# A two-layer diffusion backbone on one core: generated state-space weights made earlier, in joined operations, with fewer transfers

## The chip, the cores and the metric

One core of one Trainium2 chip runs the whole program. The metric is the device time of one execution in microseconds (us). Before the change the median of three runs is 1579.98 us (1578.12 to 1581.42). Times of the trace are counted from the first instruction.

## The reference

The model has width 1024, 512 latent tokens and 256 context tokens, and two post-norm layers. Layer 0 is windowed attention (16 query heads, 4 key heads, 128 wide), layer 1 a bidirectional state-space mixer (S5): 128 groups of 16 channels, each with 64 complex states and two directions, followed by a gated linear unit. In both layers the input projection also yields a gate path z, and the output is projected back and normalised:

```python
for i in range(DEPTH):
    h = x * (1.0 + scale) + shift            # the same for the context hc
    pz = h @ w_in
    p, z = pz[..., :-E_WIDTH], pz[..., -E_WIDTH:]
    y = attention_mixer(p) if i == 0 else s5_mixer(p)
    x = layer_norm(alpha * x + gate * ((y * silu(z)) @ w_out[i]))
# inside s5_mixer, for each direction rev:
abar = exp(lam * dt); bbar = ((abar - 1.0) / lam)[..., None] * bmat
h_t = abar * h_{t-1} + bbar @ u_t            # complex, per group
y = d * u + sum over rev of real(cmat @ h_t)
```

The parameters of the state-space layer (lam, step, B, C, D) are inputs, so the matrices made of them must be computed in the kernel.

## The kernel before, in words

**Numbers.** Large products are made of three passes in a reduced format: each operand is split into a high and a low part (`load_split`, lines 138 to 147: ScalarE rounds, VectorE subtracts), and `mm3` (lines 153 to 157) does high x high, high x low, low x high. A projection weight is loaded as one 512 KB chunk (`wchunk`, line 149) by SyncE at line 144, with two buffers for the raw chunk and two each for the parts.

**The state-space layer by chunks of 8 tokens.** Inside a chunk the recurrence is unrolled, so the kernel needs three families of matrices made from the parameters, the generated weights. All are written to DRAM and read back in layer 1:
- `gen_w` (lines 856 to 877), 64 weights: the input of a chunk to its state. One weight loads, for each direction, the tiles gE (from esc, line 865) and gB (from bt, line 867), makes two products (lines 873, 874) and a difference and a sum (lines 875, 876), and stores gW to wsc (line 877). POOL (the GpSimd engine) computes all of it. gE and gB have three buffers each, gW two.
- `gen_o` (lines 880 to 937), 32 weights of two groups each: state to output. It loads gcb and gpp, makes by, bx and bb (lines 900 to 902), and for each direction o and x and their sum (lines 912 to 914), which goes to osc in two stores a direction (line 918). POOL does it, but for q < 14 every fourth q goes to VectorE (`DO`, `DQ`).
- `lag`, inside `gen_o` (lines 920 to 936): the products of state-to-output with input-to-state for the 15 lags inside a chunk, on TensorE (lines 927 to 929, three matmuls for each of four column groups of 32; each matmul is two instructions in the trace). ScalarE and VectorE copy the result to gK, VectorE adds the D term in line 933, and it goes to ksc (line 934). Every eighth q starts 8 transfers that spread it to m0sc.

The tables esc and ppsc, which these read, come from `discretise` and `powers` (lines 713 to 853), whose arithmetic runs on VectorE in the first 190 us, beside the modulation (`ada_first`, `ada_late`) and the first projections.

**Where it runs.** `main` (lines 1315 to 1532) traces the attention layer (`layer0`) as 48 steps n, one per head pair and block of 128 tokens, plus what is needed ahead of it: `head(0)`, the first key, value and query projections in ten pieces, beside which `ada_late` loads modulation weights and multiplies with them. After each step `bg(n)` adds background work. Step 0 finishes `discretise`; steps 1 to 27 hold the 64 gen_w; steps 28 to 47 hold 14 gen_o. The next 10 gen_o are added in the first five calls of `side` during layer 0's output projection (`outproj0`), the last 8 in the first three blocks of `instate`, where layer 1 makes its chunk states from wsc. Each lag product is traced one gen_o late. Layer 1's `outstate` reads osc and m0sc.

**What sets the order.** A planner orders the instructions of each engine when the program is built: it plays the program with a model of durations and takes, on each engine, the ready instruction of best priority. `tc.high_priority(offset=-80)` (GP) puts the background 80 instructions back, -50 (LP) the lag products. The engines then execute their queues strictly in that order, and SyncE's queue, which issues nearly all transfers (the weights of line 144 and those of gen_w and gen_o alike), waits at each transfer for what that transfer needs.

Of the kernel before, what the change touches and what calls it, by code (L numbers as in the profile page):

```python
# [44 lines left out]
def prep(x, c, ctx, c_ctx, ada_w, ada_b, ln_g, ln_b, w_out, attn_w_in, attn_sink,  # L45
         s5_w_in, s5_lam_re, s5_lam_im, s5_log_step, s5_b_re, s5_b_im, s5_c_re, s5_c_im,
         s5_d, s5_glu_w, s5_glu_b, **_):
    a = consts()
# [53 lines left out]
    a["bt"] = bt.transpose(3, 1, 5, 0, 2, 4)  # L102
# [5 lines left out]
    a["cb"] = np.concatenate([a["cb"].reshape(32, 128, 512), dd], 2)  # L108
# [25 lines left out]
class K:  # L134
# [197 lines left out]
def layer0(k, bg, late):  # L332
# [380 lines left out]
def discretise(k, pool, sub):  # L713
# [56 lines left out]
    with sub("disc2") as p:  # L770
# [6 lines left out]
        for d in range(2):  # L777
            for t0 in (0, 4):
# [13 lines left out]
                for r in range(2):  # L792
                    for h in range(2):
                        nc.sync.dma_start(k.esc[d, t0:t0 + 4, :, r, h].rearrange("t i p -> i t p"),
                                          Et[64 * h:64 * h + 64, :, r, :])
# [60 lines left out]
def gen_w(k, pool, i):  # L856

    nc, a = k.nc, k.a
    eng = nc.vector if i % DW == DW - 1 else nc.gpsimd
    W = pool.tile([128, 2, 2, 2, 64], F32, name="gW", bufs=2)  # L860
    for d in range(2):
        E = pool.tile([128, 2, 2, 64], F32, name="gE", bufs=3)
        B = pool.tile([128, 2, 2, 64], F32, name="gB", bufs=3)
        e = k.esc[d, 0, i]
        nc.sync.dma_start(E, bass.AP(tensor=e.tensor, offset=e.offset, ap=[[64 * 256, 8], [0, 16], [1, 256]]))
        b = a["bt"][i, d]
        nc.sync.dma_start(B, bass.AP(tensor=b.tensor, offset=b.offset, ap=[[0, 8], [256, 16], [1, 256]]))
        m1 = pool.tile([128, 2, 2, 64], F32, name="gm1", bufs=2)
        m2 = pool.tile([128, 2, 2, 64], F32, name="gm2", bufs=2)

        def eb(r):
            return E[:, r][:, None].to_broadcast([128, 2, 2, 64])
        eng.tensor_tensor(m1, B, eb(0), op=ALU.mult)  # L873
        eng.tensor_tensor(m2, B, eb(1), op=ALU.mult)  # L874
        eng.tensor_tensor(W[:, d, :, 0], m1[:, 0], m2[:, 1], op=ALU.subtract)  # L875
        eng.tensor_tensor(W[:, d, :, 1], m1[:, 1], m2[:, 0], op=ALU.add)
    nc.sync.dma_start(k.wsc[i], W.rearrange("p d a r q -> p d (a r q)"))


def gen_o(k, pool, q):  # L880
# [4 lines left out]
    cbd = pool.tile([128, 528], F32, name="gcb", bufs=2)  # L885
    nc.sync.dma_start(cbd, a["cb"][q])
    cb = cbd[:, 0:512].rearrange("p (t d g n) -> p t d g n", t=4, d=2, g=4)
    pp = pool.tile([128, 2, 80], F32, name="gpp", bufs=2)
    nc.sync.dma_start(pp, k.ppsc[q])
    O = []  # L890
    bb = pool.tile([128, 8, 2, 16], F32, name="gbb", bufs=2)
    by = pool.tile([128, 2, 4, 16], F32, name="gby")
    bx = pool.tile([128, 2, 4, 16], F32, name="gbx")
# [9 lines left out]
    for d in range(2):  # L903
        o = pool.tile([128, 4, 9, 16], F32, name="gO", bufs=3)
        x = pool.tile([128, 4, 9, 16], F32, name="gX", bufs=1)

        def cc(t):
            return cb[:, t, d][:, :, None].to_broadcast([128, 4, 9, 16])

        def pb(o_):  # L910
            return pp[:, d, o_:o_ + 36].rearrange("p (g k) -> p g k", g=4)[:, :, :, None].to_broadcast([128, 4, 9, 16])
        eng.tensor_tensor(o, cc(0), pb(0), op=ALU.mult)  # L912
        eng.tensor_tensor(x, cc(1), pb(36), op=ALU.mult)  # L913
        eng.tensor_tensor(o, o, x, op=ALU.add)  # L914
# [5 lines left out]
    def lag():  # L920
# [16 lines left out]
    return lag  # L937
# [11 lines left out]
def gen_dram(k, dp, kind=None):  # L949
    k.esc = dp.tile([2, 8, 64, 2, 2, 64], F32, name="esc")  # L950
    k.ppsc = dp.tile([32, 128, 2, 80], F32, name="ppsc")
    k.wsc = dp.tile([64, 128, 2, 256], F32, name="wsc")
    k.osc = dp.tile([64, 128, 2, 2, 128], F32, name="osc")
# [185 lines left out]
def outstate(k, ib, X, ahead=None):  # L1139
# [4 lines left out]
    for g4 in range(0, 8, 4):  # L1144
        ps = k.ps.tile([128, 4, 128], F32, name="yps", tag="yp", bufs=2)
        for j in range(4):
# [5 lines left out]
            nc.sync.dma_start(O, k.osc[ib * 8 + g4 + j])  # L1152
# [152 lines left out]
N0, NW = 1, 28  # L1305
QO, QN = 24, 3
QA, NB = 14, 5
# [7 lines left out]
def main(tc, a):  # L1315
# [14 lines left out]
    with contextlib.ExitStack() as es:  # L1330
# [16 lines left out]
        with contextlib.ExitStack() as e2:  # L1347
# [34 lines left out]
            k.qp = Q("qp")  # L1382
            lags = []


            def out_q(upto, flush):
                nonlocal nq
                while nq < upto:
# [3 lines left out]
                    if len(lags) > 1:  # L1392
                        with tc.high_priority(offset=-LP):
                            lags.pop(0)()
                while flush and lags:
                    lags.pop(0)()

            def bg(n):
# [6 lines left out]
                elif n < NW:  # L1405
# [3 lines left out]
                    for i in range((n - N0) * 64 // (NW - N0), (n - N0 + 1) * 64 // (NW - N0)):  # L1409
                        with tc.high_priority(offset=-GP):  # L1410
                            gen_w(k, gw, i)
# [5 lines left out]
            layer0(k, bg, k.ada_late())  # L1417
# [8 lines left out]
        with contextlib.ExitStack() as e2:  # L1426
# [10 lines left out]
            gw = opener(e4)("go2", side="right")  # L1437
            nb = 0
# [111 lines left out]
```

## Time and profile before

| | before |
|---|---|
| median of 3 runs | 1579.98 us |
| the profiled execution, own time | 1584.47 us |
| its span, first to last instruction | 1582.7 us |
| TensorE (PE) busy | 1440.4 us (91%) |
| VectorE (DVE) busy | 1031.6 us (65%) |
| ScalarE (ACT) busy | 647.4 us (41%) |
| POOL busy | 650.3 us (41%) |
| mean granted clock of TensorE | 0.958 |
| DMA, hardware queue of SyncE | 59.0% of 16 engines' span |

Busy time is the union of the instructions of an engine; matmuls overlap, so a busy TensorE is not one at its peak. The clock is a share of full speed (2.4 GHz); in the records it is 1.0 or 0.5 in each stretch, 0.5 being 1.2 GHz. A wait is idle time of an engine ahead of an instruction, with the instruction that ended it. The first 90 us are the modulation and the first projections, to 706 us runs the attention layer, to 912 its output projection, to about 1164 the states of layer 1, and then the rest of layer 1.

### The profile page before, as it was taken

To read this page: it belongs to the slowest core of one execution; us is meant where nothing else is said; L and a number is where in the kernel's file an instruction comes from. 1 tells how busy PE (TensorE), PEld (TensorE's weight loads), DVE (VectorE), ACT (ScalarE), POOL (GpSimd) and SP (SyncE) were. 2 spreads that over 40 slices of the span, in tenths; PEclk is the share of its full clock that TensorE was granted. 3 is DMA by queue.
4 is the path that set the end of the run, shared out by engine and by line. 5 is a ranking of instruction groups with operands and counts; after the bars stand their busy time and mean duration, and the time that the engine had idled before them with its cause. 6 is when DMAs were issued, how large, how long until landed. Compare 5 with 4: busy or idle time off the path is not lost.

```text
span 1582.7 us, 26680 instructions
## 1 busy us (share of the span) xinstructions
PE 1440.4 (91%) x9348; PEld 1169.9 (74%) x9348; DVE 1031.6 (65%) x2679; ACT 647.4 (41%) x1256; POOL 650.3 (41%) x798
## 2 busy tenths in 40 slices
PE   7999999988997949978989799979989989999997
PEld 2545889977886848866767787768878767788876
DVE  7744666763655437775659920988888987565466
ACT  1211656644455425452223324334557355343220
POOL 0000079888999876655885545520000000000230
PEclk9999999998998969999999899989999999999999
DMA  9665455555565553587686477687766876655541
GB/s 338 213 197 177 96 168 181 183 175 183 169 191 189 168 163 120 159 242 212 185 254 193 147 244 224 198 245 240 241 212 198 288 253 221 212 187 168 184 150 57
DMA packets 270789, 309.64 MB, mean 196 GB/s; under 512 B 47296, under 2 KB 186176, under 8 KB 270656
## 3 DMA queue, kind: packets, MB, share of 16 engines
q1 hardware_dynamic: 245312, 295.37, 59.0%
q10 hardware_dynamic: 25344, 12.59, 2.8%
q8 instruction: 73, 1.20, 0.3%
q14 instruction: 60, 0.49, 0.1%
HBM read 239.20 MB, written 77.07 MB: 200 GB/s over the span
## 4 chain that ended last, share of the span: by engine, by line
PE 50%; DMA 18%; DVE 11%; POOL 10%; issue 4%; ACT 4%; SPq 2%; DVEq 0%; POOLq 0%; ACTq 0%
DMA wsc<-gW 3%; PE pg L155 3%; PE adaps L166 3%; PE pg L157 3%; PE pg L156 3%; DMA wr<-wout 3%; PE ins L1056 3%; DMA gB<-bt 2%; POOL gm L873 2%; POOL gm L874 2%; DMA gr<-gsc 2%; PE yps L1114 2%; ACT X L1099 2%; PE pq L156 2%; PE pq L155 2%
## 5 line engine op out<-in xcount | busy, mean ns | idle before, releaser
L146 DVE TENSOR_TENSOR wl<-wr,wh 128x1024 fp32r<-128x1024 f32 x104 | 132.0, 1270 | 183.0 <-ACT wh L145 182.7
L145 ACT ACTIVATE wh<-wr 128x1024 fp32r<-128x1024 f32 x104 | 109.9, 1058 | 263.5 <-DMA wr<-w 75.7
L1290 POOL TENSOR_TENSOR xt<-xt,lng 128x512 f32<-128x512 f32 (+1 forms) x9 | 12.8, 1431 | 488.1 <-DMA xt<-n0sc 488.1
L873 POOL TENSOR_TENSOR gm<-gB,gE 128x256 f32<-128x256 f32 x128 | 110.2, 861 | 185.1 <-DMA gB<-bt 185.0
L155 PE MATMUL pg<-ga,wh 128*128 128x512 f32 x256 | 100.7, 393 | 1.9 <-ACT wh L145 1.9
L874 POOL TENSOR_TENSOR gm<-gB,gE 128x256 f32<-128x256 f32 x128 | 101.7, 795 | 0.0
L157 PE MATMUL pg<-ga,wl 128*128 128x512 f32 x256 | 100.6, 393 | 0.5 <-DVE wl L146 0.5
L914 POOL TENSOR_TENSOR gO<-gO,gX 128x576 f32<-128x576 f32 x58 | 92.6, 1596 | 2.2
L912 POOL TENSOR_TENSOR gO<-gcb,gpp 128x576 f32<-128x576 f32 x58 | 75.5, 1304 | 27.1 <-PE lag L927 19.3
L1079 DVE TENSOR_TENSOR x<-m 128x64 f32<-128x64 f32 x376 | 82.5, 239 | 2.5
L488 DVE TENSOR_TENSOR ptl<-PT,pth 128x512 fp32r<-128x512 f32 (+1 forms) x96 | 60.7, 639 | 33.3 <-ACT pth L487 32.7
L913 POOL TENSOR_TENSOR gX<-gcb,gpp 128x576 f32<-128x576 f32 x58 | 78.5, 1354 | 1.9
L875 POOL TENSOR_TENSOR gW<-gm,gm 128x128 f32<-128x128 f32 x128 | 71.0, 555 | 14.9 <-DMA wsc<-gW 14.4
L927 PE MATMUL lag<-gO,gbb 128*32 128x128 f32 x256 | 42.8, 313 | 36.0 <-POOL gO L914 31.2
L462 ACT ACTIVATE P<-P,nm 128x512 f32<-128x512 f32 (+1 forms) x64 | 49.5, 774 | 62.6 <-DVE nm L446 62.3
L900 POOL TENSOR_TENSOR gby<-gcb,gpp 128x128 f32<-128x128 f32 x29 | 14.4, 496 | 147.1 <-DMA gcb<-cb 94.3
L484 PE MATMUL PT<-ident,P 128*128 128x128 f32 x352 | 61.8, 287 | 8.3 <-DVE vl L389 5.1
L146 DVE TENSOR_TENSOR gl<-gr,gh 128x512 fp32r<-128x512 f32 x48 | 49.4, 1033 | 28.6 <-ACT gh L145 28.6
L155 PE MATMUL pq<-hh,wh 128*128 128x512 f32 x160 | 65.5, 410 | 2.8 <-ACT hh L256 2.8
L468 ACT ACTIVATE P<-P,es 128x512 f32<-128x512 f32 (+2 forms) x96 | 60.9, 681 | 15.4 <-DVE es L466 15.0
L155 PE MATMUL S<-kh,qh 128*128 128x256 f32 (+1 forms) x160 | 51.9, 325 | 15.6 <-DVE nm L446 9.3
L156 PE MATMUL pq<-hl,wh 128*128 128x512 f32 x160 | 65.3, 408 | 0.8 <-DVE hl L257 0.8
(314 smaller groups left out, 4853.6 us busy)
## 6 DMA issues: line engine op xcount, KB each, us to landing
wr<-w SPq DMA_DIRECT2D x40, 512.0 KB
gE<-esc SPq DMA_DIRECT2D x128, 128.0 KB
gB<-bt SPq DMA_DIRECT2D x128, 128.0 KB
wsc<-gW SPq DMA_DIRECT2D x64, 256.0 KB
osc<-gO SPq DMA_DIRECT2D x128, 128.0 KB
wr<-wout SPq DMA_DIRECT2D x32, 512.0 KB
W<-wsc SPq DMA_DIRECT2D x32, 512.0 KB
om<-osc SPq DMA_DIRECT2D x64, 256.0 KB
```

The source lines that it names most:

```text
L145: nc.scalar.activation(hi, raw, AF.Copy)
L146: nc.vector.tensor_sub(lo, raw, f32(hi))
L155: mm(out, wh, mh, start=start, stop=False)
L156: mm(out, wh, ml, start=False, stop=False)
L157: mm(out, wl, mh, start=False, stop=stop)
L873: eng.tensor_tensor(m1, B, eb(0), op=ALU.mult)
L874: eng.tensor_tensor(m2, B, eb(1), op=ALU.mult)
L875: eng.tensor_tensor(W[:, d, :, 0], m1[:, 0], m2[:, 1], op=ALU.subtract)
L912: eng.tensor_tensor(o, cc(0), pb(0), op=ALU.mult)
L913: eng.tensor_tensor(x, cc(1), pb(36), op=ALU.mult)
L914: eng.tensor_tensor(o, o, x, op=ALU.add)
L1079: nc.vector.tensor_add(x, m[:, :, 0], m[:, :, 1])
```

## The change

**Ahead of the attention steps.** Eight gen_w (`EW`) are traced beside the ten pieces of `head(0)`, by the new callback `early`. Their tiles are borrowed from the attention layer: gE and gB lie in pth and ptl, the other three in one zs tile. `ada_late`, which used zs tiles for every second group of loads, uses qh and ql (four buffers each) instead.

**gen_w.** Both directions are in one operation: four POOL operations in place of eight, of twice the length, and two loads in place of four, of twice the size. esc and bt are laid out for that. The buffer counts stay, so that three of gE and gB now hold three weights instead of one and a half. All 64 stay on POOL.

**When.** The other 56 gen_w are in steps 1 to 21 (`NW` = 22). Steps 22 to 47 hold 27 gen_o (`QA`), the first three calls of `side` the other five (`NB` = 3, `QO` = 32), and `instate` holds none.

**gen_o.** The D terms come as their own array dd, loaded once per pool by `open_o`, not with every gcb. The two stores of a direction are one. by and bx lie inside the tile gX. In layer 0's pool gO has four buffers instead of three (`gob`).

**lag.** Four matmuls of 128 columns for direction 1, one per column group, then four for direction 0, each complete in itself, in place of three per column group that partly add up in the same columns. The term that was added up in the product is added by a second VectorE operation of 16 columns. Where gO has four buffers, and except for those flushed at the end of the layer, the first of these matmuls gets an order edge behind the last POOL (or VectorE) operation of the following gen_o; it orders them for the planner and adds no semaphore wait on the chip.

```diff
@@ ada_late, load
-                    z = [self.qp.tile([128, 2, 768], F32, name="zs", bufs=2) for _ in range(2)]
-                    ws = [t[:, i, 0:512] for t in z for i in range(2)]
+                    ws = [f32(self.qq.tile([128, 768], F32R, name=n, bufs=4))[:, 0:512] for n in ("qh", "ql", "qh", "ql")]
@@ layer0
-    for _ in head(0):
+    for j, _ in enumerate(head(0)):
         for i in range(2):
             next(late, None)
+        early(j)
@@ gen_w
+def w_tiles(k, pool):
+    sh = [128, 2, 2, 2, 64]
+    if pool is not None:
+        return [pool.tile(sh, F32, name=n, bufs=b) for n, b in (("gE", 3), ("gB", 3), ("gm1", 1), ("gm2", 1), ("gW", 2))]
+    eb = [f32(k.sp.tile([128, 2, 2, 128], F32R, name=n, bufs=2)).rearrange("p d r (a q) -> p d r a q", a=2)
+          for n in ("pth", "ptl")]
+    z = k.qp.tile([128, 2, 768], F32, name="zs", bufs=2).rearrange("p h q -> p (h q)")
+    return eb + [z[:, 512 * i:512 * i + 512].rearrange("p (d r a q) -> p d r a q", d=2, r=2, a=2) for i in range(3)]
-    for d in range(2):
-        E = pool.tile([128, 2, 2, 64], F32, name="gE", bufs=3)
-        B = pool.tile([128, 2, 2, 64], F32, name="gB", bufs=3)
...
-        eng.tensor_tensor(m1, B, eb(0), op=ALU.mult)
-        eng.tensor_tensor(m2, B, eb(1), op=ALU.mult)
-        eng.tensor_tensor(W[:, d, :, 0], m1[:, 0], m2[:, 1], op=ALU.subtract)
-        eng.tensor_tensor(W[:, d, :, 1], m1[:, 1], m2[:, 0], op=ALU.add)
+    E, B, m1, m2, W = tiles
...
+    tt = nc.gpsimd.tensor_tensor
+    tt(x(m1), x(B), eb(0), op=ALU.mult)
+    tt(x(m2), x(B), eb(1), op=ALU.mult)
+    tt(W[:, :, :, 0], m1[:, :, 0], m2[:, :, 1], op=ALU.subtract)
+    tt(W[:, :, :, 1], m1[:, :, 1], m2[:, :, 0], op=ALU.add)
@@ gen_o
+def open_o(k, pool, q0, q1, gob):
+    k.gob, k.dq = gob, q0
+    k.dd = pool.tile([128, 16 * (q1 - q0)], F32, name="dd")
+    k.nc.sync.dma_start(k.dd, k.a["dd"][:, 16 * q0:16 * q1])
...
-        o = pool.tile([128, 4, 9, 16], F32, name="gO", bufs=3)
+        o = pool.tile([128, 4, 9, 16], F32, name="gO", bufs=k.gob)
...
-        for u in range(2):
-            nc.sync.dma_start(k.osc[2 * q + u, :, :, d], o[:, 2 * u:2 * u + 2, x0:x0 + 8].rearrange("p r t n -> p r (t n)"))
+        nc.sync.dma_start(k.osc[q, :, :, :, d].rearrange("p u r x -> p (u r) x"),
+                          o[:, :, x0:x0 + 8].rearrange("p g t n -> p g (t n)"))
@@ lag
-        for g in range(4):
-            rs = slice(32 * g, 32 * g + 32)
-            nc.tensor.matmul(ps[rs, 0:128], lh(1, g), O[1][:, g, 1:9], start=True, stop=False)
-            nc.tensor.matmul(ps[rs, 112:128], lh(0, g), O[0][:, g, 0], start=False, stop=True)
-            nc.tensor.matmul(ps[rs, 128:240], lh(0, g), O[0][:, g, 1:8], start=True, stop=True)
+        for d in (1, 0):
+            for g in range(4):
+                rs = slice(32 * g, 32 * g + 32)
+                m = nc.tensor.matmul(ps[rs, 128 * (1 - d):128 * (1 - d) + 128], lh(d, g), O[d][:, g, d:d + 8], start=True, stop=True)
+                if g == 0 and d == 1 and after is not None and k.gob > 3:
+                    k.tc.add_manual_dep(ins_of(m), ins_of(after).name,
+                                        mybir.DependencyInfo(mybir.DependencyClass.NoSync, mybir.DependencyReason.DATA), reason="lag")
...
-        nc.scalar.activation(K_[:, 128:240], ps[:, 128:240], AF.Copy)
-        nc.vector.tensor_add(K_[:, 112:128], ps[:, 112:128], cbd[:, 512:528])
+        nc.scalar.activation(K_[:, 128:240], ps[:, 144:256], AF.Copy)
+        nc.vector.tensor_add(K_[:, 112:128], ps[:, 112:128], dd[:, 16 * (q - k.dq):16 * (q - k.dq) + 16])
+        nc.vector.tensor_add(K_[:, 112:128], ps[:, 128:144], K_[:, 112:128])
@@ constants, main
-N0, NW = 1, 28
-QO, QN = 24, 3
-QA, NB = 14, 5
+N0, NW, EW = 1, 22, 8
+QO, QN = 32, 1
+QA, NB = 27, 3
...
-                            lags.pop(0)()
+                            lags.pop(0)[0](lags[-1][1])
...
+            def early(j):
+                gens(EW * (j + 1) // 10, None)
...
+                        open_o(k, gw, 0, QA, 4)
...
+            open_o(k, gw, QA, 32, 3)
```

## Rows read from the trace of the kernel before

**Rows 1.** Stretches cut at the stages: span us, busy us per engine (instructions), clock, DMA share, GB/s
```profile
90.00:197.00 107.00, 106.56 (x619) 68.73 (x618) 51.63 (x160) 34.78 (x73) 0.00 (x0) 1.00 0.52 158
197.00:320.00 123.00, 121.17 (x815) 110.92 (x813) 84.20 (x193) 74.83 (x173) 105.32 (x163) 1.00 0.56 174
320.00:600.00 280.00, 230.21 (x1420) 206.28 (x1419) 138.36 (x294) 126.53 (x301) 245.81 (x375) 0.90 0.57 176
600.00:706.00 106.00, 96.78 (x774) 85.61 (x773) 83.12 (x164) 58.96 (x154) 63.63 (x57) 0.97 0.60 178
706.00:912.00 206.00, 177.72 (x1009) 143.00 (x1007) 146.58 (x216) 60.01 (x113) 133.26 (x108) 0.92 0.66 198
912.00:1060.00 148.00, 134.71 (x1211) 112.92 (x1208) 76.35 (x168) 49.85 (x90) 74.74 (x72) 0.95 0.71 220
```

**Rows 2.** The page's chain that ended last, shares of the span by engine
```profile
PE 50%; DMA 18%; DVE 11%; POOL 10%; issue 4%; ACT 4%; SPq 2%; DVEq 0%; POOLq 0%; ACTq 0%
```

**Rows 3.** TensorE's waits, 320 to 600 us: us in total, times, longest
```profile
PE lag L927 <- POOL gO L914: 15.6, 1, 15.6
...
PE vt L387 <- ACT vT L381: 7.2, 2, 6.3
```

**Rows 4.** SyncE's queue waits, 320 to 600 us: us in total, times, longest
```profile
SPq L865 <- POOL gm L874: 85.8, 63, 3.2
```

**Rows 5.** Instructions on esc, source view: ns min/median/max, first and last start us
```profile
L865 SPq DMA_DIRECT2D gE<-esc x128: 577/594/713, 197.5 to 557.2; - x128
...
L794 SPq DMA_DIRECT2D esc<-Et x16: 574/608/905, 66.4 to 85.0; - x16
```

**Rows 6.** Line 873, source view: ns min/median/max, first and last start us
```profile
L873 POOL TENSOR_TENSOR gm<-gB,gE x128: 719/739/1802, 202.1 to 565.1; 128x256 f32<-128x256 f32 x128
```

**Rows 7.** Groups by line, POOL: busy us, mean ns | idle before
```profile
L873 POOL TENSOR_TENSOR gm<-gB,gE 128x256 f32<-128x256 f32 x128 | 110.2, 861 | 185.1 <-DMA gB<-bt 185.0
...
L874 POOL TENSOR_TENSOR gm<-gB,gE 128x256 f32<-128x256 f32 x128 | 101.7, 795 | 0.0
...
L875 POOL TENSOR_TENSOR gW<-gm,gm 128x128 f32<-128x128 f32 x128 | 71.0, 555 | 14.9 <-DMA wsc<-gW 14.4
...
L876 POOL TENSOR_TENSOR gW<-gm,gm 128x128 f32<-128x128 f32 x128 | 64.3, 502 | 0.0
...
L900 POOL TENSOR_TENSOR gby<-gcb,gpp 128x128 f32<-128x128 f32 x29 | 14.4, 496 | 147.1 <-DMA gcb<-cb 94.3 <-DMA gpp<-ppsc 47.3 <-DMA osc<-gO 5.5
...
L901 POOL TENSOR_TENSOR gbx<-gcb,gpp 128x128 f32<-128x128 f32 x29 | 15.0, 517 | 0.0
...
L902 POOL TENSOR_TENSOR gbb<-gby,gbx 128x256 f32<-128x256 f32 x29 | 25.5, 880 | 0.0
...
L912 POOL TENSOR_TENSOR gO<-gcb,gpp 128x576 f32<-128x576 f32 x58 | 75.5, 1304 | 27.1 <-PE lag L927 19.3 <-DMA osc<-gO 7.7 <-PE pul L157 0.2
...
L913 POOL TENSOR_TENSOR gX<-gcb,gpp 128x576 f32<-128x576 f32 x58 | 78.5, 1354 | 1.9
...
L914 POOL TENSOR_TENSOR gO<-gO,gX 128x576 f32<-128x576 f32 x58 | 92.6, 1596 | 2.2
```

**Rows 8.** TensorE's timeline, one lag product: start us, us; its first row, the next work
```profile
606.67 0.41 PE L927 MATMUL lag<-gO,gbb 128*32 128x128 f32 x2
...
608.01 0.33 PE L484 MATMUL PT<-ident,P 128*128 128x128 f32 x1
```

**Rows 9.** The chain in order of time: start us, us, what
```profile
1176.63 1.90 PE yps L1114 x32
```

**Rows 10.** TensorE's waits, 690 to 920 us
```profile
PE lag L927 <- POOL gO L914: 10.5, 4, 4.3
...
PE lag L927 <- DVE gK L933: 4.4, 1, 4.4
```

**Rows 11.** TensorE's waits, 920 to 1060 us
```profile
PE lag L927 <- POOL gO L914: 5.1, 2, 3.7
...
PE ins L1056 <- DMA V<-vsc: 4.9, 2, 4.0
```

More of the change, by code (lines that the diff above doesn't have):

```diff
@@ L329, with layer0 @@
 Z0, Z1 = 1, 1
-def layer0(k, bg, late):
+def layer0(k, bg, early, late):
     tc, nc, a = k.tc, k.nc, k.a
@@ L793, in discretise @@
                     for h in range(2):
-                        nc.sync.dma_start(k.esc[d, t0:t0 + 4, :, r, h].rearrange("t i p -> i t p"),
+                        nc.sync.dma_start(k.esc[t0:t0 + 4, :, d, r, h].rearrange("t i p -> i t p"),
                                           Et[64 * h:64 * h + 64, :, r, :])
@@ new lines, in gen_w, with eb, x @@
+def gen_w(k, tiles, i):
+    nc, a = k.nc, k.a
+    E, B, m1, m2, W = tiles
+    e = k.esc[0, i]
+    nc.sync.dma_start(E.rearrange("p d r a q -> p (d r a q)"),
+                      bass.AP(tensor=e.tensor, offset=e.offset, ap=[[64 * 512, 8], [0, 16], [1, 512]]))
+    b = a["bt"][i]
+    nc.sync.dma_start(B.rearrange("p d r a q -> p (d r a q)"),
+                      bass.AP(tensor=b.tensor, offset=b.offset, ap=[[0, 8], [512, 16], [1, 512]]))
+    def eb(r):
+        return E[:, :, r].rearrange("p d a q -> p d (a q)")[:, :, None].to_broadcast([128, 2, 2, 128])
+    def x(t):
+        return t.rearrange("p d r a q -> p d r (a q)")
+    tt = nc.gpsimd.tensor_tensor
[3 more added lines that the diff above has]
+    tt(W[:, :, :, 1], m1[:, :, 1], m2[:, :, 0], op=ALU.add)
@@ L884, in gen_o @@
     eng = nc.vector if q % n == n - 1 else nc.gpsimd
-    cbd = pool.tile([128, 528], F32, name="gcb", bufs=2)
-    nc.sync.dma_start(cbd, a["cb"][q])
-    cb = cbd[:, 0:512].rearrange("p (t d g n) -> p t d g n", t=4, d=2, g=4)
+    cb = pool.tile([128, 4, 2, 4, 16], F32, name="gcb", bufs=2)
+    nc.sync.dma_start(cb.rearrange("p t d g n -> p (t d g n)"), a["cb"][q])
     pp = pool.tile([128, 2, 80], F32, name="gpp", bufs=2)
     nc.sync.dma_start(pp, k.ppsc[q])
+    dd = k.dd
     O = []
     bb = pool.tile([128, 8, 2, 16], F32, name="gbb", bufs=2)
-    by = pool.tile([128, 2, 4, 16], F32, name="gby")
-    bx = pool.tile([128, 2, 4, 16], F32, name="gbx")
+    t = pool.tile([128, 4, 9, 16], F32, name="gX", bufs=1).rearrange("p g k n -> p (g k n)")
+    by, bx = (t[:, 128 * i:128 * i + 128].rearrange("p (d g n) -> p d g n", d=2, g=4) for i in range(2))
     def qb(o):
@@ L913, in gen_o, with lag @@
         eng.tensor_tensor(x, cc(1), pb(36), op=ALU.mult)
-        eng.tensor_tensor(o, o, x, op=ALU.add)
+        last = eng.tensor_tensor(o, o, x, op=ALU.add)
         O.append(o)
         x0 = 1 - d
-        for u in range(2):
-            nc.sync.dma_start(k.osc[2 * q + u, :, :, d], o[:, 2 * u:2 * u + 2, x0:x0 + 8].rearrange("p r t n -> p r (t n)"))
-    def lag():
+        nc.sync.dma_start(k.osc[q, :, :, :, d].rearrange("p u r x -> p (u r) x"),
+                          o[:, :, x0:x0 + 8].rearrange("p g t n -> p g (t n)"))
+    def lag(after=None):
         ps = k.ps.tile([128, 512], F32, name="lag", tag=k.lagtag[0], bufs=k.lagtag[1])
@@ L936, in lag, with ins_of @@
             gen_m0(k, q // 8)
-    return lag
+    return lag, last
+def ins_of(i):
+    return getattr(i, "ins", i)
 def gen_m0(k, qr):
@@ L949, in gen_dram @@
 def gen_dram(k, dp, kind=None):
-    k.esc = dp.tile([2, 8, 64, 2, 2, 64], F32, name="esc")
+    k.esc = dp.tile([8, 64, 2, 2, 2, 64], F32, name="esc")
     k.ppsc = dp.tile([32, 128, 2, 80], F32, name="ppsc")
     k.wsc = dp.tile([64, 128, 2, 256], F32, name="wsc")
-    k.osc = dp.tile([64, 128, 2, 2, 128], F32, name="osc")
+    k.osc = dp.tile([32, 128, 2, 2, 2, 128], F32, name="osc")
     k.ksc = dp.tile([32, 128, 240], F32, name="ksc")
@@ L1151, in outstate @@
             O = om_tile(k, [128, 2, 2, 128], bool(ahead))
-            nc.sync.dma_start(O, k.osc[ib * 8 + g4 + j])
+            nc.sync.dma_start(O, k.osc[(ib * 8 + g4 + j) // 2, :, j % 2])
             yps_mm(k, ps, j, [(X[:, d, par, i], O[:, par, d]) for d in range(2) for par in range(2)], bool(ahead), True)
@@ L1393, in out_q, with gens @@
                         with tc.high_priority(offset=-LP):
-                            lags.pop(0)()
+                            lags.pop(0)[0](lags[-1][1])
                 while flush and lags:
-                    lags.pop(0)()
+                    lags.pop(0)[0]()
+            def gens(upto, pool):
+                nonlocal nw
+                while nw < upto:
+                    with tc.high_priority(offset=-GP):
+                        gen_w(k, w_tiles(k, pool), nw)
+                    nw += 1
+            def early(j):
+                gens(EW * (j + 1) // 10, None)
             def bg(n):
@@ L1408, in bg @@
                         gw = opener(e4)("gw")
-                    for i in range((n - N0) * 64 // (NW - N0), (n - N0 + 1) * 64 // (NW - N0)):
-                        with tc.high_priority(offset=-GP):
-                            gen_w(k, gw, i)
+                    gens(EW + (64 - EW) * (n + 1 - N0) // (NW - N0), gw)
                 else:
```

18 lines of the change are left out of this document (4 added, 14 removed).

## The prediction

> **What bounds the kernel now.** I read the stages first, then the chain, then the waits of the two queues that the change touches, then what one generated weight costs. In the stages [rows 1] TensorE is busy almost without a break from 90 to 320 us (1.8 us idle of 123 in the second stretch), loses 49.8 of 280 us from 320 to 600, 9.2 of 106 to the end of the attention layer at 706, 28.3 of 206 in its output projection and 13.3 of 148 while the first chunks of the state-space layer are made. The clock says the same a second time: 0.90 from 320 to 600, so 56 us lay at the lower level (1.2 GHz), against 1.00 before. A microsecond of products done at that level costs half a microsecond more; as some of the 56 us are idle anyway, the price is between 3 us (all idle inside) and 28 us (none), and I take 16. In the chain [rows 2] TensorE has half of the span, but DMA and POOL together 28%, which is a lot for engines that only make weights for later. The reader should ask how POOL can hold TensorE at all, since the attention layer never reads these weights.
>
> The queue of SyncE answers it. From 320 to 600 us it stood 85.8 us, 63 times, on POOL [rows 4]: a load of gE (line 865) waits until POOL has freed the buffer, and the projection weights (line 144) are behind it on the same queue. Each such load also costs 0.59 us of issue [rows 5], four of them a weight with the B loads. So TensorE's single waits carry other names [rows 3], and only one, 15.6 us, names POOL: the first lag product, issued before its operand was made. POOL works from 202.1 to about 567.5 us on the 64 weights of gen_w (line 873 starts last at 565.1, three operations follow), 5.71 us each [rows 6]; its instructions are 2 x (0.861 + 0.795 + 0.555 + 0.502) = 5.43 us of that [rows 7].
>
> **The change, part by part.** The sum is made against the profiled execution: span 1582.7, own time 1584.5 us, 4.5 above the median of 1580.0.
>
> **Lag products.** 24 instructions on TensorE become 16, and the same columns now go round four column groups instead of staying in one for three in a row. One lag product holds TensorE 1.34 us (606.67 to 608.01) [rows 8], 56 ns an instruction, though they are of 16, 112 and 128 columns alike: that is a price by instruction, not by column. The products of 128 columns that alternate between two column groups take 1.90 us for 32, 59 ns each [rows 9], so full-width ones keep that pace. 16 x 56 ns = 0.90 us, 0.44 less, x 32 = **14 us** less. If columns decide, nothing is saved (their number is the same); bounds 0 and 14. The Trainium skill, "TensorE: Matmul & The Clock Gate", Part 3 (measured speedup vs the span model), states that matmuls in different column groups run side by side at some 4 ns a further one; as an estimate from that page one lag product would take about 0.5 us, the saving would be 27 us and the forecast 1507. No row here shows four groups in turn, and the two that alternate [rows 9] are no faster than today's order, so I stay with the 56 ns.
>
> **POOL's work.** One gen_w becomes four operations of twice the length. For 512 elements I go between the rows of 256 (0.83 on average) and 576: 1.23 us by the broadcast ones (1.304, 1.354), 1.44 by the one with two full inputs (1.596) [rows 7]. The new operands are full ones: 2 x 1.44 + 2 x 0.83 = 4.5 us, with 0.15 of waits 4.65 a weight instead of 5.71. Eight go ahead, beside the first projections; 56 are left: 260 us against 365, so the first gen_o starts near 465 instead of 570. But 27 of the gen_o weights, not 14, are then made in the attention layer. Three of either go to VectorE. One on POOL is 0.496 + 0.517 + 0.880 + 2 x (1.304 + 1.354 + 1.596) = 10.4 us. POOL's total there: before 365 + 11 x 10.4 = 480, after 260 + 24 x 10.4 = 510 us, where TensorE has 706 - 197 = 509. POOL is full to the end of the layer.
>
> **The attention layer.** Until 320 us some 21 weights cost TensorE nothing; the next 43 cost 34.2 us of idle (49.8 less the 15.6) and about 16 of clock, 1.16 us a weight. After: 35 past the first 21, with half the loads and three whole weights of prefetch instead of one and a half; I take 0.8 each, 28, so 22 less. The first lag product is now queued one weight (10.4 us) later: 10 of its 15.6 us go. The denser gen_o has no row; at 60% POOL load TensorE lost 9.2 of 106 us [rows 1], and I charge 10 more. Sum **22 us** less. Bounds: 78 less, if all idle and clock loss of 320 to 706 goes (49.8 + 9.2 + 16 + 3); 30 more, if the 30 us that POOL has on top comes whole. What is late next is again SyncE behind POOL, now at the osc stores (line 918).
>
> **The output projection.** Five gen_o instead of ten; lag waits of 10.5 + 4.4 us [rows 10], and 0.08 x 206 = 16 us by the clock. In the second pool no order is forced, and POOL may come in late from the layer: I take half, **15 us**. Bounds 0 and 31.
>
> **The first chunks.** The last eight weights leave this stage. Their lag waits (5.1) and the late V load (4.9) [rows 11], part of 13.3 idle and 7.4 by the clock, go: **12 us**, bounds 5 and 21. The lag products themselves are only moved.
>
> **Beside the first projections.** Eight weights add 24 DMAs on SyncE and some 37 us of POOL where TensorE had 0.4 us of idle in 107 and POOL nothing [rows 1]. The esc stores issue by 85.0 us [rows 5], so the data is there; VectorE is half free. At the price of a late weight of today (1.16) it is 9 us, at none 0: **3 us** more. The modulation weights only change buffers (more of them). The own load of D (one DMA a pool), the second addition of 16 columns and the joined osc stores (64 issues fewer) lie beside TensorE's work; without that cover they are under 10 us together, inside the bounds.
>
> Sum: 14 + 22 + 15 + 12 - 3 = 60 us. 1584.5 - 60 = 1524.5; a median lies 4.5 lower: **1520**. All low bounds: 0 - 30 + 0 + 5 - 9 = 34 slower; all high: 14 + 78 + 31 + 21 = 144 faster.
>
> **The rivals.** **Full cover** (chance 0.20): fewer loads and deeper buffers free SyncE, and from 320 on TensorE runs as from 197 to 320, where POOL was as busy (105 of 123 us) and nothing was lost. For it: that stretch. Against: 43 of 64 weights did cost something. The layer gives 65, the projection 22, the chunks 15, with 14 for the products: 116 less, 1464.
> **POOL paces the layer** (0.17): 510 us fill 509, every late POOL operation is passed on, and the order edge, which makes nothing wait on the chip and holds in the first pool alone, helps little. The layer gets 10 longer; the projection gives 10, the chunks 12, the products 14, less 3: 23 less, 1557.
> **Slower** (0.10): POOL was busy 88% of 320 to 600 us. At that share its 510 us take 580 and end at 777, not 706. If the last lag products of the layer stand ahead of the output projection on TensorE, that is 71 us on the path; 14, 15 and 12 come back: 30 slower, 1610. It decides once POOL ends more than some 41 us after today's 706; against it speaks that TensorE has a whole projection to do meanwhile.
> **Nothing** (0.03): the waits only change their names, 1580.
>
> **Numbers.** The forecast has 0.50. A change of 0.2% (3 us) is about what a measurement of this kernel can tell. The first three cases are faster, 0.87; 0.03 the same; 0.10 slower. The range, 1470 to 1572, leaves out the slow case and the deeper half of full cover.
>
> **What would show it.** Right: line 873 (its successor) ends before 480 us with under 4.7 us a weight; SyncE's waits on POOL there are under half of 85.8; the lag group has 512 instructions and some 0.9 us each time; no POOL work after about 830 us; TensorE's idle from 912 on under 5 us. Wrong: new lag waits of 10 us or more between 600 and 800 us with a fallen clock behind them, idle TensorE before 200 us, or W operations over 5.2 us a weight.

## The result and the profile after

The changed kernel takes 1511.39 us (median of 4 runs, 1508.89 to 1513.09), against 1580.7 us (1578.12 to 1584.35, 4 runs) before: a ratio of 0.9547, with a 95% interval of 0.9516 to 0.9577. That is 69 us, or 4.5%. The profiled execution took 1508.89 us, its span is 1507.1 us. The mean granted clock of TensorE rose from 0.958 to 0.971.

First the stretches of [rows 1] again, with the same columns (length, then busy us and instructions of PE, PEld, DVE, ACT, POOL, the granted clock, the DMA share and GB/s):

```profile
90.00:197.00 107.00, 104.01 (x602) 68.06 (x601) 59.98 (x170) 35.92 (x79) 35.45 (x32) 1.00 0.64 187
197.00:320.00 123.00, 118.97 (x771) 108.12 (x770) 85.99 (x173) 67.81 (x156) 113.44 (x101) 0.97 0.65 206
320.00:600.00 280.00, 257.13 (x1765) 227.69 (x1764) 187.52 (x385) 152.35 (x377) 229.95 (x206) 0.96 0.59 182
600.00:706.00 106.00, 92.61 (x604) 77.39 (x604) 81.50 (x135) 49.98 (x120) 97.72 (x81) 0.92 0.72 217
706.00:912.00 206.00, 179.75 (x1120) 147.49 (x1121) 144.11 (x220) 64.33 (x124) 124.11 (x100) 0.93 0.68 206
912.00:1060.00 148.00, 148.00 (x1360) 123.69 (x1356) 103.89 (x513) 67.58 (x121) 0.00 (x0) 1.00 0.69 221
```

From 320 to 600 us TensorE is idle for 22.9 us where it was 49.8, and its clock is 0.96 instead of 0.90. From 912 to 1060 us POOL has nothing to do and TensorE has no idle time at all. Before 320 us there is a small price: 7.0 us idle (2.99 + 4.03) against 2.3.

Fixed stretches now cover other work, so stages are better cut by what starts them. In the tile view of TensorE a stage begins with the first product of S (attention), of po<-woh (output projection; its few products on wh start 3.4 us earlier here and up to 8.4 us earlier in the other kernels), of puc (first chunks) and of yps (second half of layer 1); the last two figures ahead of the semicolon are the first and the last start:

```profile
L155 PE MATMUL S<-kh,qh x160: 277/283/580, 138.1 to 644.3; 128*128 128x256 f32 x128, 128*128 128x384 f32 x32
L155 PE MATMUL po<-woh,gh x156: 282/389/796, 673.7 to 857.1; 128*128 128x512 f32 x132, 128*128 128x256 f32 x24
L155 PE MATMUL puc<-H1H,wh x128: 274/281/390, 857.5 to 1047.6; 128*128 128x256 f32 x128
L1142 PE MATMUL yps<-om,V x256: 272/273/323, 1089.2 to 1254.7; 128*64 128x128 f32 x128
```

Worked out in the same way for every kernel (po starts at 713.1 us before, puc at 905.9, yps at 1159.6, and the span ends at 1582.7):

| stage | before | changed | difference |
|---|---|---|---|
| start to po | 713.1 | 673.7 | -39.4 |
| po to puc | 192.8 | 183.8 | -9.0 |
| puc to yps | 253.7 | 231.7 | -22.0 |
| yps to the end | 423.1 | 417.9 | -5.2 |

Idle times given for a stage below are its length less TensorE's busy time in it. The last line of the table was in no term of the forecast and was not looked into. Together the four are the 75.6 us between the two spans. It is more than the 69 of the medians because the profiled execution before lay 3.8 us above its median and the one after 2.5 below.

The chain that ended last has less of TensorE and of DMA, and more of POOL and VectorE, than [rows 2]:

```profile
PE 45%; POOL 16%; DVE 15%; DMA 13%; issue 5%; ACT 4%; SPq 1%; POOLq 0%; ACTq 0%; DVEq 0%
```

A generated weight costs about what was worked out for it. In the groups of POOL (busy us, mean ns, idle before):

```profile
L886 POOL TENSOR_TENSOR gm<-gB,gE 128x512 f32<-128x512 f32 x56 | 84.1, 1503 | 0.0
...
L885 POOL TENSOR_TENSOR gm<-gB,gE 128x512 f32<-128x512 f32 x56 | 79.3, 1416 | 23.5 <-DVE zs L500 19.2
...
L888 POOL TENSOR_TENSOR gW<-gm,gm 128x256 f32<-128x256 f32 x56 | 49.4, 883 | 0.0
L887 POOL TENSOR_TENSOR gW<-gm,gm 128x256 f32<-128x256 f32 x56 | 46.8, 836 | 9.7 <-DMA wsc<-gW 6.2
```

The four means sum to 4.64 us a weight, against 5.43 in [rows 7] and 4.5 in the forecast. The source view of line 885, which took the place of line 873 in [rows 6], gives the times:

```profile
L885 POOL TENSOR_TENSOR gm<-gB,gE x56: 1267/1296/2168, 201.0 to 465.9; 128x512 f32<-128x512 f32 x56
L885 POOL TENSOR_TENSOR zs<-ptl,pth x8: 1275/1292/2260, 110.4 to 176.4; 128x512 f32<-128x512 f32 x8
```

Eight weights are done by about 182 us, and the other 56 by 470 us, not 568. From 201.0 us to the end of the last one at 470 that is 4.8 us a weight, against 5.71 before and 4.65 forecast. The timeline of TensorE shows a lag product as one row (start, length, then the row of the next work):

```profile
497.68 0.65 PE L948 MATMUL lag<-gO,gbb 128*32 128x128 f32 x16
498.25 0.39 PE L155 MATMUL S<-kh,qh 128*128 128x256 f32 x1
```

It holds TensorE from 497.68 to 498.25, 0.57 us, where it held 1.34 in [rows 8]: 36 ns an instruction.

### The profile page after: what moved, and what is told of

It is laid out like the page before. It is cut to its first block, busy times and chain, and to the rows that moved or that the text cites. A ratio compares the mean times of both kernels' runs of the same rounds, so it can differ in the third digit from the quotient of the medians.

```text
span 1507.1 us, 25647 instructions
## 1 busy us (share of the span) xinstructions
PE 1401.6 (93%) x9092; PEld 1130.5 (75%) x9092; DVE 1048.1 (70%) x2711; ACT 645.3 (43%) x1256; POOL 628.3 (42%) x542
## 4 chain that ended last, share of the span: by engine, by line
PE 45%; POOL 16%; DVE 15%; DMA 13%; issue 5%; ACT 4%; SPq 1%; POOLq 0%; ACTq 0%; DVEq 0%
PE pg L155 4%; PE pg L157 4%; PE pg L156 4%; PE adaps L166 3%; DMA wsc<-gW 3%; POOL gm L886 3%; POOL gm L885 3%; DMA wr<-wout 3%; PE ins L1084 3%; POOL gW L888 3%; DMA gr<-gsc 2%; PE pul L155 2%; PE pul L156 2%; POOL gW L887 2%; PE pul L157 2%
## 5 line engine op out<-in xcount | busy, mean ns | idle before, releaser
L146 DVE TENSOR_TENSOR wl<-wr,wh 128x1024 fp32r<-128x1024 f32 x104 | 140.9, 1355 | 144.1 <-ACT wh L145 133.0
L931 POOL TENSOR_TENSOR gO<-gcb,gpp 128x576 f32<-128x576 f32 x58 | 79.2, 1370 | 29.4 <-PE lag L948 21.5
L885 POOL TENSOR_TENSOR gm<-gB,gE 128x512 f32<-128x512 f32 x56 | 79.3, 1416 | 23.5 <-DVE zs L500 19.2
L886 POOL TENSOR_TENSOR gm<-gB,gE 128x512 f32<-128x512 f32 x56 | 84.1, 1503 | 0.0
L1107 DVE TENSOR_TENSOR x<-m 128x64 f32<-128x64 f32 x376 | 74.1, 215 | 2.4
L155 PE MATMUL po<-woh,gh 128*128 128x512 f32 (+1 forms) x156 | 60.3, 396 | 8.0 <-ACT woh L580 8.0
L486 ACT ACTIVATE pth<-PT 128x512 fp32r<-128x512 f32 (+1 forms) x96 | 52.4, 558 | 33.9 <-PE PT L483 25.8
L156 PE MATMUL po<-wol,gh 128*128 128x512 f32 (+1 forms) x156 | 61.9, 398 | 5.3 <-DVE wol L581 5.3
L157 PE MATMUL pq<-hh,wl 128*128 128x512 f32 x160 | 66.0, 412 | 0.3 <-DVE wl L146 0.3
```

Of the source, the lines that this page charges most:

```text
L146: nc.vector.tensor_sub(lo, raw, f32(hi))
L155: mm(out, wh, mh, start=start, stop=False)
L156: mm(out, wh, ml, start=False, stop=False)
L157: mm(out, wl, mh, start=False, stop=stop)
L885: tt(x(m1), x(B), eb(0), op=ALU.mult)
L886: tt(x(m2), x(B), eb(1), op=ALU.mult)
```

## The experiments

Three questions were open: which of the parts brings the time, through which wait, and what the new placement (8 weights early, 27 gen_o in the attention layer) is worth. The rival to a sum of parts was that one part makes all of it, and that the rest moves work about. Each time below is a median, and each ratio compares with runs of the kernel before on the same chip. Kernels of different experiments ran on three chips; the median of the kernel before lay between 1579.57 and 1583.4 us there, so a difference of a few us between two experiments means nothing.

**1. Only the lag products as before.** The changed kernel with the three matmuls a group, the one addition, and the order edge kept:

```diff
-        for d in (1, 0):
-            for g in range(4):
...
-                m = nc.tensor.matmul(ps[rs, 128 * (1 - d):...], lh(d, g), O[d][:, g, d:d + 8], ...)
...
+        for g in range(4):
...
+            m = nc.tensor.matmul(ps[rs, 0:128], lh(1, g), O[1][:, g, 1:9], ...)
...
+            nc.tensor.matmul(ps[rs, 112:128], lh(0, g), O[0][:, g, 0], ...)
+            nc.tensor.matmul(ps[rs, 128:240], lh(0, g), O[0][:, g, 1:8], ...)
```

> The changed kernel with the old lag products (three matmuls per column group, one addition; the order edge kept). One regrouped lag product holds TensorE 0.57 us in the changed kernel's trace, an old one 1.34. Theory A, TensorE is the bound and every microsecond of lag products is on the path: 32 x 0.77 = 25 us slower than the changed kernel, 1536. Theory B, the saved time is lost in waits for POOL in the attention layer, where most lag products lie: under 10 us slower, 1511 to 1521.

Measured: 1536.49 us (1532.31 to 1538.79), ratio 0.9724 [0.97, 0.9749], so 25 us more than the changed kernel. That is 32 x 0.77 us, but the stages say that it isn't simply that. Up to puc, where 28 of the 32 products run, only 8 us are lost (865.5 against 857.5); 19 us are lost between puc and yps, where four remain. POOL's last gen_o now ends at 899.5 us instead of 871.2, and POOL stands 35 us longer on lag products that have to free its gO buffers. The waits of POOL from 470 to 1050 us in this kernel:

```profile
POOL gO L931 <- PE lag L947: 45.5, 19, 8.7
...
POOL gO L931 <- PE lag L952: 11.4, 3, 5.7
```

and in the changed kernel:

```profile
POOL gO L931 <- PE lag L948: 21.5, 8, 9.8
```

TensorE then stands in front of its last lag products (15.2 us from 690 to 920 us, two waits), which the changed kernel does not. From puc to yps its idle time is 20.8 us against 9.1. So the number fits the first theory and the stages do not: most of the loss comes through POOL's lateness. That the longer products alone make POOL wait, and not another order that the planner found with them, is a reading; no run separates the two.

**2. Only the lag products regrouped.** The kernel before with the loop of the change and its second addition.

> The kernel before with the regrouped lag products alone. Theory A: 25 us faster than before, 1556, the lag group at 0.57 us each. Theory B (POOL paces the layer): 5 to 12 us faster, 1569 to 1576, since the products stand beside POOL-bound work.

Measured: 1583.42 us (1574.2 to 1590.02, 10 runs), ratio 1.0025 [1.0005, 1.0046]: no gain. TensorE is relieved as in the changed kernel, as the timeline shows (601.44 to 602.02, 0.58 us):

```profile
601.44 0.64 PE L928 MATMUL lag<-gO,gbb 128*32 128x128 f32 x16
602.02 0.39 PE L156 MATMUL O<-ptl,vh 128*128 128x256 f32 x1
```

Neither theory's time came. The products still start 8 to 15 us apart in the attention layer, at the pace of POOL's gen_o, and POOL waits from 470 to 1100 us less for lag products (19.8 us, 19.3 before) than for its own loads:

```profile
POOL gby L900 <- DMA gcb<-cb: 84.9, 15, 14.7
```

TensorE's idle time does not fall where most of the products lie (63.3 us from S to po against 63.7, 33.8 from po to puc against 25.9). The profiled execution was the quickest of the ten, 9 us under the median. It is 4.9 us shorter up to po and 13.9 from puc to yps, and 9.3 longer after yps. So up to puc the saved time went mostly into other waits; where the median loses the rest is open.

**3. Only gen_w joined** (the kernel before with the four operations, two loads and whole-weight buffers of the change, at the old place).

```diff
+    sh = [128, 2, 2, 2, 64]
...
-    for d in range(2):
-        E = pool.tile([128, 2, 2, 64], F32, name="gE", bufs=3)
...
-        eng.tensor_tensor(m1, B, eb(0), op=ALU.mult)
...
+    E, B, m1, m2, W = tiles
...
+    tt(x(m1), x(B), eb(0), op=ALU.mult)
```

> The kernel before with both directions of gen_w in one operation and two loads instead of four, at the old places. Theory A, SyncE's queue behind POOL's gen_w holds TensorE in the attention layer: POOL is through with gen_w near 510 instead of 568 us, the idle of 320 to 600 (49.8 us) halves, 30 us faster, 1550. Rival, gen_w is off the path and its waits only change names: at most 5 us faster, 1575 to 1580.

Measured: 1536.18 us (1534.61 to 1538.87), ratio 0.9727 [0.9705, 0.9749], 44 us less than before. With the 25 of experiment 1 this makes 69, the whole difference. Of the 49 us between the two spans 27 come back ahead of po (685.9 us against 713.1), with idle time from S to po of 32.4 us against 63.7, and 17 from po to puc.

**4 to 6. Which part of the join.** Three cuts of it, each on the kernel before: whole-weight loads but eight operations (per-direction slices of the same tiles), joined operations but a load for each direction, and nothing but six buffers for gE and gB.

```diff
+    for d in range(2):
+        tt(x(m1)[:, d], x(B)[:, d], eb(0)[:, d], op=ALU.mult)     # joined loads only
...
+        nc.sync.dma_start(E[:, d]..., ap=[[64 * 512, 8], [0, 16], [1, 256]])     # joined operations only
...
-        E = pool.tile([128, 2, 2, 64], F32, name="gE", bufs=3)
+        E = pool.tile([128, 2, 2, 64], F32, name="gE", bufs=6)     # depth only
```

> The kernel before with gen_w's loads and buffers joined (two loads a weight, three weights of prefetch) but eight POOL operations a weight, one set per direction. Joined whole, gen_w gave 44 us (1536). If the transfers and the queue are the cause: 30 us or more faster than before, at most 1550. If POOL's time in its operations is the cause (5.43 us a weight against 4.61): at most 15 us faster, 1565 to 1580.

> The kernel before with joined POOL operations and the deep buffers (three whole weights), but each weight still loaded by four transfers of 128 KB. If the depth of the buffers is what the joined loads brought: 1535 to 1550, and ScalarE's waits for the projection weights from 300 to 570 us under 20 us (62.6 before, 15.1 with joined loads). If the number of transfers on SyncE's queue is: at most 15 us faster than before, 1565 to 1580, and those waits above 40 us.

> The kernel before with six buffers each for gE and gB instead of three, nothing else: three whole weights of prefetch, four transfers, eight POOL operations. Depth theory: 1540 to 1550. Transfer-count theory: within 10 us of before, 1570 to 1580.

Measured: joined loads 1540.15 us (1539.54 to 1544.28), ratio 0.976 [0.9737, 0.9783]; joined operations 1542.05 (1538.66 to 1543.89), 0.9751 [0.9723, 0.9779]; depth alone 1567.03 (1561.6 to 1568.66), 0.9902 [0.9866, 0.9939]. Depth alone brings 15 us, between the forecasts of its two theories. A kernel with the depth and either join gains about 40 in all, and with both 44: the joins do the same job twice. The wait that follows the time is not on POOL or SyncE but on ScalarE, which rounds the projection weights that queue behind these loads on SyncE. SyncE itself stands longer with joined loads than before (111.4 us on POOL's gm from 300 to 570 us, against 93.7). ScalarE's waits for them from 300 to 570 us (us in total, times, longest), first before:

```profile
ACT wh L145 <- DMA wr<-w: 62.6, 11, 11.5
```

with depth alone:

```profile
ACT wh L145 <- DMA wr<-w: 53.2, 12, 7.5
```

with joined loads:

```profile
ACT wh L145 <- DMA wr<-w: 15.1, 5, 4.9
```

with joined operations:

```profile
ACT wh L145 <- DMA wr<-w: 4.1, 1, 4.1
```

and in the changed kernel:

```profile
ACT wh L145 <- DMA wr<-w: 2.9, 1, 2.9
```

In experiment 3 it is 9.8 us. Of these kernels all with 15.1 us or less of it gain 39 us or more, and the one that keeps 53.2 gains 15. The wait is a sign and not a price, though: the kernel of experiment 2 has 50.1 and gained nothing. How fast POOL is hardly matters: with joined loads gen_w ends at 546 us, with joined operations at 510, and the two times agree. Why either join is enough, although one leaves four transfers a weight and the other eight operations, no run separates. Both also have buffers for whole weights and the new layout of esc and bt, which depth alone has not.

**7. No order edge.** The changed kernel with the edge of the lag products switched off (`k.gob > 9`).

> The changed kernel without the order edge behind the next weight's last POOL operation. If the edge keeps lag products from being issued too early: lag waits of 10 to 20 us more in the attention layer and a fallen clock behind them, 1520 to 1530. If it does nothing (an order that the planner finds anyway): 1511 within 3 us.

Measured: 1516.98 us (1509.33 to 1519.32), ratio 0.9596 [0.9564, 0.9627], 6 us more, between its two theories, with intervals that overlap the changed kernel's. The trace shows what the edge does. TensorE's waits from 320 to 690 us without it:

```profile
PE lag L948 <- POOL gO L933: 26.6, 8, 14.3
```

and with it, from 320 to 600 us (there is no further one to 690), the row that answers to the first of [rows 3]:

```profile
PE lag L948 <- POOL gO L933: 9.3, 1, 9.3
```

Without the edge, po starts 15 us later (688.4 against 673.7), but no lag product is left for the chunks, and the stretch from puc to yps is 10.8 us shorter. The edge mostly moves the cost.

**8 to 10. The placement.** The changed kernel with no early weights; the changed kernel at the old place altogether; and the kernel before with the new place of gen_o alone.

```diff
-N0, NW, EW = 1, 22, 8
+N0, NW, EW = 1, 22, 0     # no early weights
...
+N0, NW, EW = 1, 28, 0     # old place: 14, 10 and 8 gen_o
+QO, QN = 24, 3
+QA, NB = 14, 5
...
-N0, NW = 1, 28     # kernel before, new place
...
+N0, NW = 1, 22
+QO, QN = 32, 1
+QA, NB = 27, 3
```

> The changed kernel without the eight early weights: all 64 gen_w in steps 1 to 21. POOL then has 8 x 4.8 = 38 us more between 197 us and the first gen_o, which starts near 515 instead of 475. If POOL's progress sets the attention layer: 15 to 30 us slower than the changed kernel, 1526 to 1541. If TensorE has enough other work there: within 4 us of 1511.

> All new parts (joined gen_w, new lag products, own D terms, fewer stores, the order edge) at the places of before: 64 gen_w in steps 1 to 27, 14, 10 and 8 gen_o, none early. If the parts make the gain (joined gen_w alone gave 44, lag products on top 25): 1508 to 1518, as the changed kernel. If the placement makes it, or if the lag products pay only where the new placement puts them (alone they gave nothing): 1530 to 1540.

> The kernel before with the new places alone: 64 gen_w in steps 1 to 21, 27 gen_o in steps 22 to 47, 5 in the output projection, none early, nothing joined. POOL's work there is 365 + 250 us and ends near 820. If POOL paces what is beside it: no faster, 1575 to 1600, the attention layer longer by what the chunk stage gets shorter. If the gain lies in the emptied chunk stage: 20 us faster, 1560.

Measured: no early weights 1548.89 us (1541.54 to 1549.28), 0.9795 [0.9761, 0.9828], 37 more than the changed kernel and more than either theory had. The old place 1512.81 (1508.89 to 1515.18), 0.9579 [0.9553, 0.9606], within 2 us of it, with intervals that overlap. The new place with the old parts 1610.85 (1606.4 to 1610.92), 1.0196 [1.0172, 1.022], 31 slower than before and again outside both theories. So the placement nets nothing with the new parts: the dense gen_o cost 36 us (1548.89 less 1512.81), and the eight early weights pay them back. Where that cost lies the first kernel shows in its stretch from 706 to 912 us, at a clock of 0.83 and with 65 us idle,

```profile
706.00:912.00 206.00, 141.11 (x826) 109.44 (x825) 136.52 (x216) 52.44 (x105) 151.62 (x131) 0.83 0.60 180
```

and in the last kernel TensorE's waits for POOL, from 690 to 920 us:

```profile
PE lag L927 <- POOL gO L914: 19.7, 6, 4.7
```

and from 920 to 1160 us:

```profile
PE lag L927 <- POOL gO L914: 25.2, 3, 12.4
```

POOL's last gen_o ends at 913.2 us without the early weights and at 871.2 with them.

The stages, cut as above, say where each kernel has its time:

| stage | join alone (3) | no early (8) | old place (9) | place alone (10) |
|---|---|---|---|---|
| start to po | 685.9 | 667.3 | 662.6 | 707.3 |
| po to puc | 175.7 | 195.0 | 177.6 | 205.3 |
| puc to yps | 252.0 | 266.7 | 247.2 | 271.9 |
| yps to the end | 420.3 | 418.5 | 426.0 | 424.6 |

The dense gen_o costs 4.7 us ahead of po (667.3 against 662.6) and 37 from po to yps. The changed kernel reaches po 6.4 us later than without its early weights and then gains 46 up to yps. Against experiment 3 the old place gains another 23 us, by the lag products and the small parts of gen_o together. The small parts (own D terms, joined stores, fourth gO buffer) were not tried alone; but with all of them, the new placement and the old lag products (experiment 1, 1536.49) the time is that of the join alone (1536.18).

**11 and 12. More of the early weights.** Twelve instead of eight; and twelve with gen_w and gen_o spread wider (`N0, NW, EW = 1, 24, 12`, `QA, NB = 24, 5`).

> The changed kernel with 12 early weights instead of 8. Without the eight it was 37 us slower, since POOL fell behind. If POOL is still the pace: it ends some 19 us earlier and the kernel gains 4 to 10 us, 1501 to 1507. If eight are enough, or the early stage has no room for more (TensorE had 0.4 us of idle in 107 there): 1510 to 1520.

> The changed kernel with 12 early weights, the others over steps 1 to 23, 24 gen_o in steps 24 to 47 and 8 in the first five calls of the output projection. If POOL's lateness at the end of the attention layer and in the output projection is what is left: 1495 to 1506. If the work merely moves: 1508 to 1518.

Measured: 1518.74 us (1516.87 to 1520.88), 0.9607 [0.9581, 0.9633], and 1528.04 (1525.43 to 1534.06), 0.967 [0.9638, 0.9703]; both lose, 7 and 17 us, the second more than either of its theories had. The early weights use the buffers of the attention's own tiles (pth, ptl, zs). With twelve, the last start at 203 us, and ScalarE's first pth waits for them, as its waits from the start to 320 us show:

```profile
ACT pth L486 <- POOL zs L886: 22.7, 2, 20.8
```

TensorE stands 24.9 us behind that (its first O product). In the changed kernel that wait of ScalarE is 2.4 us (two times), so eight fit in these buffers and twelve do not; no number between was tried. No version tried beats the changed kernel.

## Why the prediction was right, and where its terms were off

The total was right (1520 predicted, 1511.39 measured, inside 1470 to 1572), and so was the case named as likeliest: late projection weights behind SyncE, relieved in part. The terms were not all right, and that the total came so near is partly luck: by stage, with the lag products at 0.44 us, the forecast was 26 less up to po, 21 from po to puc, 13 from puc to yps and nothing after, and 39.4, 9.0, 22.0 and 5.2 came.

**Lag products: the step that failed is the price by instruction.** The forecast took 56 ns for each of the 16 (0.90 us). They take 36 (0.57 us). The estimate from the Trainium skill, "TensorE: Matmul & The Clock Gate", Part 3 (measured speedup vs the span model), where column groups run side by side, was about 0.5 us; this trace is nearer to it than to the row. The row that was taken as nearest, two alternating groups at 59 ns [rows 9], was no guide to four. The second half of the step was wrong too: it put the saving straight on the path. Alone it brought nothing (experiment 2), and with the rest of the change 25 us, of which 8 lie ahead of puc and the rest where POOL's lateness is made up (experiment 1).

**The attention layer: mis-sized.** It forecast 22 less there, 3 more ahead of it, and, at 0.44 us, 7 less for the 17 lag products that fall before po: 26. Up to po 39.4 went. The late weights went nearly entirely, 62.6 to 2.9 us, where 0.8 us for each further weight (28 in all) was kept. What stayed has the denser gen_o beside it (clock 0.92 and 13.4 us idle from 600 to 706 us). It was charged at 10 us here; experiments 8 and 9 put 4.7 ahead of po, and the larger part behind it.

**Beside the first projections: under-sized.** Idle time is 4.7 us more up to 320 us; at a clock of 0.97 over 123 us, 7 us lay at the lower level (1.2 GHz), up to 4 us more. The first S product comes at 138.1 us, without the early weights at 129.3 (experiment 8), before the change at 127.8. The forecast was 3, with 9 as its end; what came is nearer to 9. The buffers' limit, which experiment 11 found between eight and twelve, was not seen.

**The output projection: over-sized.** 15 was forecast on top of the lag products. 9.0 came, and 12 products at 1.34 us against 13 at 0.57 are 8.7 of it. Of the waits and the clock nothing was won: 26.5 us idle against 25.9, the clock 0.92 in both. POOL is late there as foreseen, but the wait that took the place of [rows 10]'s lag waits is another. TensorE, 690 to 920 us:

```profile
PE h1t L1013 <- DVE nrm L631: 19.5, 7, 6.0
PE po L155 <- ACT woh L580: 8.0, 3, 5.1
```

The first was 4.7 us before:

```profile
PE h1t L985 <- DVE nrm L631: 4.7, 4, 3.3
```

What holds VectorE there, in part at least, is told in the last section.

**The first chunks: under-sized.** 12 was forecast and the lag products were called only moved; 22 came. Six of eight of them left this stage (2 remain; 8 x 1.34 against 0.57 and 1.01 us, so 9 us), and the rest is mostly idle time (16.3 to 9.1 us) and clock (0.97 to 0.98).

**The signs.** Right were line 885's end (465.9, under 480), 512 lag instructions and, from 912 to 1060 us, no idle TensorE; after 1060 us it is idle 23.5 us, 27.5 before. A weight takes 4.64 us by its operations but 4.8 by the clock of the trace, so "under 4.7" just failed. POOL's last gen_o ended at 871.2 us, not by 830. One sign was wrong in principle: SyncE's waits on POOL in [rows 4] were to halve from 85.8 us. From 320 to 600 us the row that answers to it, for the loads, and those for the stores are:

```profile
SPq L873 <- POOL gm L886: 58.7, 28, 3.3
SPq L936 <- POOL gO L933: 35.6, 14, 10.1
...
SPq L889 <- POOL gW L888: 24.5, 25, 4.7
```

and the rows for the stores before:

```profile
SPq L877 <- POOL gW L876: 14.4, 19, 5.3
SPq L918 <- POOL gO L914: 10.1, 3, 7.5
```

The loads alone wait less, though not half. The three rows sum to 118.8 us, against 110.3 before, and yet the weights are on time. A queue that stands costs nothing until what lies behind it is late.

**The rivals.** *Slower* did not come. Experiment 10, the new place without the new parts, took 1610.85 us, beside its forecast of 1610, but that is chance. The rival had the last lag products of the layer stand ahead of the output projection; there po starts at 707.3 us, no later than before, and the time is lost from po to puc (205.3 us against 192.8) and from puc to yps (271.9 against 253.7). *POOL paces the layer* said 1557, and without the early weights the kernel takes 1548.89; but its layer, to be 10 us longer, is 46 us shorter up to po, and again the time goes behind po. Both were right that a late POOL is passed on, and wrong about where. *Full cover* holds for the weights, not for the layer: 36.3 us idle remain from S to po.

## What to carry to other kernels

When background loads share an in-order queue with the weights of the main path, look for lateness at the consumer's first instruction on those weights (here ScalarE's 62.6 us), not at how long the queue stands; loading and computing whole units behind deeper buffers cured it, and one of the two joins would nearly have done (about 40 of 44 us). A saving on an engine that waits anyway shows only once that wait has gone, so measure parts both alone and taken out of the whole: here one gave 0 alone and 25 taken out. Work moved earlier is bounded by the buffers that it borrows.

## What the runs showed of the hardware

Sixteen lag instructions over four column groups in turn took 0.57 us, 36 ns each, against 56 with three in a row in one group; at the lower clock (0.5) one product took about twice as long, 1.01 us (872.91 to 873.92).

More surprising was VectorE. In the norm at the end of a block it runs tiny operations on 128x1. Here is VectorE's timeline of one (start, length):

```profile
816.39 1.09 DVE L294 SCALAR_TENSOR_TENSOR nt<-nt,ih 128x1 f32<-128x1 f32 x1
817.52 1.44 DVE L293 SCALAR_TENSOR_TENSOR nt<-nt,xe 128x1 f32<-128x1 f32 x1
...
819.48 1.11 DVE L294 SCALAR_TENSOR_TENSOR nt<-nt 128x1 f32<-128x1 f32 x1
820.63 1.44 DVE L293 SCALAR_TENSOR_TENSOR nt<-nt,xe 128x1 f32<-128x1 f32 x1
```

and POOL's over the same time:

```profile
816.31 1.16 POOL L932 TENSOR_TENSOR gX<-gcb,gpp 128x576 f32<-128x576 f32 x1
817.55 1.40 POOL L933 TENSOR_TENSOR gO<-gO,gX 128x576 f32<-128x576 f32 x1
819.02 1.56 POOL L932 TENSOR_TENSOR gX<-gcb,gpp 128x576 f32<-128x576 f32 x1
820.65 1.40 POOL L933 TENSOR_TENSOR gO<-gO,gX 128x576 f32<-128x576 f32 x1
```

Each of VectorE's operations ends within 0.1 us of the end of POOL's (817.48 and 817.47, 818.96 and 818.95, 820.59 and 820.58, 822.07 and 822.05). The same lines take 0.16 and 0.22 us at their medians. The 36 such operations from 706 to 912 us sum to 23.1 us in this kernel and 15.9 before, which lies on the way to the h1t products that wait 19.5 us. The Trainium skill, "SBUF — State Buffer", who interferes with whom, has a rule for this: a VectorE instruction with two inputs in SBUF contends with a POOL instruction that reads SBUF, over a shared pair of ports that only one of them can hold. These four pairs agree; which of the two came first the starts do not tell (817.52 against 817.55 in the second), and the next VectorE operation, at 822.10, took 0.16 us although POOL's next began at 822.13. So POOL's work can have a price that no wait names: the short operations of VectorE beside it take longer. How much of the h1t waits is due to this was not tried.
